# A fixed order of instructions for the attention stage of a hybrid encoder layer

## The chip, the cores and the metric

One NeuronCore of a Trainium2 chip. The metric is the device time of one execution in microseconds (us), the median of several executions. The engines are TensorE (PE in the profile; PEld is its weight load), VectorE (DVE), ScalarE (ACT), GpSimd (POOL), and SyncE (SP), which issues most of the transfers. Each has an instruction queue of its own, and they wait for each other through semaphores.

## What is computed

One layer of an encoder over 256 frames of 2048 features, all in float32. The reference, cut to what matters here:

```python
proj = x @ w_in                       # q | k | v | u, 1024 columns each
attn = chunk_band_attention(q, k, v, rel_bias)   # 16 heads of 64
ssm  = s5_mixer(u, ...)               # 64 groups, a 64-dim complex diagonal state each
ssm  = gelu(ssm)
ssm  = ssm * sigmoid(ssm @ w_glu + b_glu)
mixed = concat([rms_norm(attn, g_attn), rms_norm(ssm, g_ssm)]) @ w_out
x = layer_norm(alpha * x + mixed)
gate = causal_depthwise_conv(x @ w_gate)
x = layer_norm(alpha * x + (gelu(gate) * (x @ w_val)) @ w_ffn_out)

# in chunk_band_attention, per head:
scores = q @ k.T * 64 ** -0.5 + bias  # banded by chunks of 64 frames
out    = softmax(scores) @ v
# in s5_mixer, per group: s[t] = a * s[t-1] + B u[t] (complex, a scan); y = Re(C s) + D u
```

## The kernel before

All products run on TensorE as float32 matmuls of a rounded high part and a low rest. The weights come in chunks of 128 x 1024 elements (512 KB). The loop in `run` takes one chunk per step, and such a step is called a block below. For block j it first splits the weights of block j + 3 (`split_chunk`, lines 163 and 164: a cast on ScalarE gives hi, a subtraction on VectorE gives lo), then issues the transfer of block j + 7 on SP (`dma_chunk`), then the matmuls of block j, then what takes the result out of PSUM (`post`), and last one step of every side generator that has started, in the order in which they were registered. There are four buffers each for raw, hi and lo.

The blocks of the first phase: 0 to 7 half of V (`mm_b`, twelve matmuls of 512 columns a block, lines 245, 247, 249), 8 to 23 U (`mm_a`, eight pairs of one matmul of 512 and one of 256 columns, lines 206 to 211), 24 to 31 the other half of V, 32 to 63 K and Q (four blocks for each pair of heads: two of K, two of Q), 64 to 79 the attention half of the output projection (oa), 80 to 87 GLU, 88 to 103 the other half of it (os). Then comes the feed-forward part, which is most of the time and isn't touched.

The side generators that matter:

- `s5_loc` (from block 16) puts state products (ll, line 778) and transposes (lt, line 762) into a queue, each with a cost. `fill`, called after most matmuls, adds 1 to a credit (at most 2) and takes from the queue while the credit is at least 1. A state product costs 0.25, so a few of them go between two matmuls.
- `s5_kstack` (from 24) puts 64 products for the kernel matrix (ks, line 873) there, at 0.5 each, into PSUM bank 2, which half of V also uses.
- `s5_cm` (from 22) builds the matrices CM on VectorE (lines 943 to 948), two steps for each of four.
- `s5_scan` (from 35) runs the scan on VectorE: 21 complex multiply-adds of four operations each (lines 844 to 847), 14 of them long (128 x 512) and 7 short (128 x 64). `paced` emits one and yields when the costs reach a budget of 1.6 per block. Then `s5_y` (lines 952 to 983) makes y on TensorE (line 973), four times two halves of one PSUM bank, each copied out by VectorE (line 974), then the GELU and the operand of GLU.
- `attention(j)` (from block 36 + 4j, j from 0 to 7): the loads of the two bands of bias, the scores of two heads (S, lines 1048 and 1049), `soft` for each head (sum and maximum on VectorE, line 1061; their negative, line 1062; exponentials on ScalarE, line 1065), `trans` (three transposes and a copy to the one pT buffer on ScalarE, lines 1071 to 1075), `pv` (products with V, lines 1084 to 1086), `norm` (lines 1090 to 1099: reciprocal and product at on VectorE, then two squares on ScalarE), and `evac` (transposes back, line 1104; scaling and attnhl on ScalarE, lines 1108 and 1109; the low part on VectorE, line 1110).

`evac_k` (line 501, kz) and `evac_q` (line 506, qt) take K and Q out of PSUM, with a copy on ScalarE first (lines 467 and 469).

What is written isn't yet the order on an engine. The framework collects the instructions, and its scheduler lets each engine take, in a time that it assumes, the earliest-written instruction that is ready. So an engine's queue may differ from the written order. On the chip, each queue then runs in the order that was set.

Of the kernel before, what the change touches and what calls it, by code (L numbers as in the profile page):

```python
# [12 lines left out]
F32 = mybir.dt.float32  # L13
# [3 lines left out]
ALU = mybir.AluOpType  # L17
# [3 lines left out]
P = 128  # L21
# [97 lines left out]
class Builder:  # L119
    def __init__(self, nc, tc, ctx, I, out):  # L120
        self.nc, self.tc, self.ctx, self.I, self.out = nc, tc, ctx, I, out
        self.chunks = []
        self.sides = []
        self.queue = deque()
        self.credit = 0.0


# [39 lines left out]
    def run(self, first=None):  # L167
        self.raw, self.hl = {}, {}
        if first is not None:
            first()  # L170
        else:
            for j in range(4):
                self.dma_chunk(j)
            for j in range(3):
                self.split_chunk(j)
                self.dma_chunk(j + 4)
        self.start()
        j = 0
        while j < len(self.chunks) or self.sides:
            self.split_chunk(j + 3)  # L180
            self.dma_chunk(j + 7)
            if j < len(self.chunks):
                hi, lo = self.hl.pop(j)
                self.chunks[j][1](hi, lo)
                if self.chunks[j][2] is not None:
                    self.chunks[j][2]()
            keep = []
            for s in self.sides:
                if s[0] <= j:
                    try:  # L190
                        with self.tc.high_priority(s[2]) if s[2] else nullcontext():
                            next(s[1])
                    except StopIteration:
                        continue
                keep.append(s)
            self.sides = keep
            j += 1


    def mm_a(self, ps, hi, lo, xs, k0, first, last, nk=8):  # L200
# [49 lines left out]
                self.fill()  # L250

    def t1(self, shape, name):
        return self.ap_.tile(shape, F32, tag="t1", bufs=6, name=name)

    def bank(self, i, name):
        return self.pp.tile([P, 512], F32, tag=f"b{i}", name=name)
# [35 lines left out]
    def plan_phase1(self):  # L292
# [163 lines left out]
        self.side(24, self.s5_kstack(), 200)  # L456
        self.side(22, self.s5_cm())
        self.side(35, self.s5_scan())
        for j in range(8):
            self.side(36 + 4 * j, self.attention(j))  # L460
        self.side(78, self.load_x())
# [290 lines left out]
    def s5_loc(self):  # L752
        nc, bp = self.nc, self.bp
        loc, put = self.loc, self.put
        st = {}

        def lt(pg, ri):
            def mm(i):
                if i == 0:
                    st[0] = self.bank((6, 7)[ri], f"lt{pg}{ri}")  # L760
                c = pg * 8 + 2 * i
                nc.tensor.transpose(st[0][:, P * i:P * i + P],
                                    self.MB[:, ri, c:c + 2].rearrange("p c e q -> p (c e q)"), self.ident)

            def evac():
                for g2 in range(2):
                    r = slice(64 * g2, 64 * g2 + 64)
                    nc.scalar.copy(loc[r, pg % 2, ri, :, r], st[0][r].rearrange("p (i n) -> p i n", n=64))
            for i in range(4):
                put(lambda i=i: mm(i))  # L770
            put(evac, 0)

        def ll(q, ri):
            def mm(i, g2):
                if i == 0 and g2 == 0:
                    st[1] = self.bank((3, 4)[ri], f"ll{q}{ri}")
                r = slice(64 * g2, 64 * g2 + 64)
                nc.tensor.matmul(st[1][r, 64 * i:64 * i + 64], lhsT=loc[:, q % 2, ri, i, r], rhs=self.up[:, q * 8 + i],
                                 start=True, stop=True, tile_position=(0, 64 * g2))

            def evac():
                v = st[1].rearrange("p (i c) -> p i c", c=64)
                nc.scalar.copy(self.X[:, ri, q * 8:q * 8 + 8, 8:64], v[:, :, 0:56])
                nc.scalar.copy(self.L8[:, ri, q * 8:q * 8 + 8], v[:, :, 56:64])
            for i in range(8):
                for g2 in range(2):
                    put(lambda i=i, g2=g2: mm(i, g2), 0.25)
            put(evac, 0)

        def both(f, pg):  # L790
            for ri in range(2):
                f(pg, ri)

        def drained():
            while self.queue:
                yield
            yield
        for pg in range(2):
            while self.mb_ready <= pg:
                yield  # L800
            yield
            both(lt, pg)
            yield
        while self.mb_ready < 4 or self.up_ready < 1:
            yield
        self.X = bp.tile([P, 2, NP_, 64], F32, tag="d2", name="X")
        nc.gpsimd.memset(self.X[:, :, :, 0], 0.0)
        yield from drained()
        yield
        both(ll, 0)  # L810
        both(lt, 2)
        yield from drained()
        both(ll, 1)
        both(lt, 3)
        yield from drained()
        self.lt_done = True
        while self.up_ready < 2:
            yield
        yield
        both(ll, 2)  # L820
        both(ll, 3)
        yield from drained()
        self.loc_done = True
        yield

    def s5_scan(self):
# [8 lines left out]
        def madd(cost, o, s, ar, ai, shape, add=None):  # L835

            n = math.prod(shape[1:])
            add = o if add is None else add

            def f():  # L840
                u, w = (self.kcm[:, c:c + n].rearrange("p (r x) -> p r x", r=2) for c in (1024, 1536))
                if len(shape) == 4:
                    u, w = (t.rearrange("p r (c b) -> p r c b", b=shape[3]) for t in (u, w))
                V.tensor_tensor(u, s[:, ::-1], ai, op=ALU.mult)
                V.tensor_tensor(w, s, ar, op=ALU.mult)
                V.tensor_tensor(u, u, add, op=ALU.add)
                V.tensor_tensor(o, w, u, op=ALU.add)
            ops.append((cost, f))
        sh = [P, 2, NP_, 8]
        one = lambda q, k: q[:, :, :, k]  # L850
        bc = lambda q, k: one(q, k).unsqueeze(3).broadcast_to(sh)
        row = lambda k: L8 if k == 8 else X[:, :, :, k]
        for k in range(2, 9):
            madd(2.7, row(k), row(k - 1), bc(QR, 0), bc(QI, 0), sh)
        for b in range(7):
            madd(1.1, X[:, :, :, 0, b + 1], X[:, :, :, 0, b], one(QR, 7), one(QI, 7), [P, 2, NP_], L8[:, :, :, b])
        for k in range(1, 8):
            madd(2.7, row(k), row(0), bc(QR, k - 1), bc(QI, k - 1), sh)
        yield from self.paced(ops, 1.6)
        yield from self.s5_y()  # L860

    def s5_kstack(self):
# [5 lines left out]

        def mm(i, ri, h):
            if not st:  # L870
                st[0] = self.bank(2, "ks")
            pr = 16 * h + i
            nc.tensor.matmul(st[0][64 * h:64 * h + 64, 32 * i:32 * i + 32],
                             lhsT=self.MB[:, ri, pr].rearrange("p e q -> p (e q)"),
# [2 lines left out]
        for i in range(16):  # L877
            for ri in range(2):
                for h in range(2):
                    self.put(lambda i=i, ri=ri, h=h: mm(i, ri, h), 0.5)  # L880
        while self.queue:
            yield
        ps = st[0]
# [152 lines left out]
    def attention(self, j):  # L1036
# [2 lines left out]
        v = self.res1  # L1039
        st = {}  # L1040

        def load(h):
            b = st["b", h] = ap.tile([P, 256], F32, tag="band", bufs=2, name=f"bd{j}{h}")
            nc.sync.dma_start(b, I["band"][2 * j + h])

        def scores(h):
            ps = st["S", h] = self.bank(5 + h, f"S{j}{h}")
            nc.tensor.matmul(ps[:, 0:256], lhsT=qt[:, P:2 * P], rhs=kz[h], start=True, stop=True)
# [1 line left out]

        def soft(h):

            ps, b = st["S", h], st["b", h]
            s = ap.tile([P, 384], F32, tag="sT", bufs=2, name=f"sT{j}{h}")
            if h == 0:
                st["m"] = ap.tile([P, 12], F32, tag="mx", bufs=2, name=f"mx{j}")
# [10 lines left out]

        def trans(h):
            s = st["s", h]
            ps = self.bank(7, f"T{j}{h}")  # L1070
            nc.tensor.transpose(ps[:, 0:128], s[:, 256:384], self.ident)
            nc.tensor.transpose(ps[:, 128:256], s[:, 0:128], self.ident)
            nc.tensor.transpose(ps[:, 256:384], s[:, 128:256], self.ident)
            pt = st["pt", h] = ap.tile([P, 384], F32, tag="pT", name=f"pT{j}{h}")
            nc.scalar.copy(pt, ps[:, 0:384])

        def pv(h):
# [10 lines left out]
        def norm():  # L1088
            m = st["m"]
            nc.vector.reciprocal(m[:, 0:4], m[:, 8:12])  # L1090
            if j == 0:
# [1 line left out]
            a = st["a"] = self.t1([P, SEQ], f"at{j}")  # L1093
            nc.vector.tensor_tensor(a.rearrange("p (g c) -> p g c", c=64), st["o"][:, 0:256].rearrange("p (g c) -> p g c", c=64),
                                    m[:, 0:4].unsqueeze(2).broadcast_to([P, 4, 64]), op=ALU.mult)
            q = self.t1([P, SEQ], f"aq{j}")
            for t in range(2):
                r = slice(P * t, P * t + P)
                nc.scalar.activation(q[:, r], a[:, r], AF.Square, accum_out=self.ssq[:, t, j:j + 1])
# [1 line left out]
        def evac():  # L1101
# [5 lines left out]
            a = self.t1([P, SEQ], f"ag{j}")  # L1107
            nc.scalar.mul(a, ps, self.pv["g_attn"][:, j:j + 1])
            nc.scalar.copy(self.attnhl[:, j, 0:SEQ], a)
            nc.vector.tensor_tensor(self.attnhl[:, j, SEQ:], a, self.attnhl[:, j, 0:SEQ].bitcast(F32), op=ALU.subtract)  # L1110

        load(0)
        load(1)
        scores(0)
        scores(1)
        yield
        soft(0)
        yield
        soft(1)
        yield  # L1120
        if j < 7:
            yield
        trans(0)
        yield
        pv(0)
        trans(1)
        if j < 7:
            yield
        pv(1)
        norm()  # L1130
        yield
        while self.cm_ready < 4:
            yield
        evac()
        yield


# [251 lines left out]
```

## Time and profile before

| | |
|---|---|
| median of 3 runs | 1140.65 us (1139.38 to 1142.46) |
| profiled execution, its own time | 1141.15 us |
| its span, first to last instruction | 1139.3 us |
| TensorE busy | 1110.3 us (97%) |
| VectorE busy | 774.4 us (68%) |
| ScalarE busy | 566.6 us (50%) |
| GpSimd busy | 75.5 us (7%) |
| mean granted TensorE clock | 0.991 |

The busy time of an engine is a share of the whole span, over stages with different limits. The granted clock is the share of the full TensorE clock that the chip allowed. The times of matmuls overlap, so what one takes is read from start to start.

### The profile page before, as it was taken

The numbers are of one execution on the slowest core, as the hardware profiler recorded it, in microseconds if no ns is written. First come the engines' busy times: TensorE is split into PE (matmuls) and PEld (weight loads), VectorE is DVE, ScalarE is ACT, GpSimd is POOL, SyncE is SP. The second block draws the span as 40 slices with busy tenths as digits, with TensorE's granted clock in tenths as the row PEclk, the third lists the DMA queues.
The fourth block names the chain that finished last, engine by engine and source line by source line (L and its number), as shares of the span: only waits on it lengthen the run. The fifth ranks groups of instructions, "written<-read, shape, count | busy, mean of one in ns | idle before, by whom it ended". The sixth has DMA issues, their size and how long they took to land.

```text
span 1139.3 us, 17905 instructions
## 1 busy us (share of the span) xinstructions
PE 1110.3 (97%) x6980; PEld 948.8 (83%) x6980; DVE 774.4 (68%) x1230; ACT 566.6 (50%) x882; POOL 75.5 (7%) x75
## 2 busy tenths in 40 slices
PE   8999979999999999999999999999999999999996
PEld 6887768888887888888888888888888888888885
DVE  7996889946588776666666666666666575454555
ACT  5455325537575565555555555555555443433350
POOL 2021300000011000000000000000000550000002
PEclk9999979999999999999999999999999999999998
DMA  8886334534766366666666666666666876666661
GB/s 303 279 226 164 118 122 139 162 96 138 244 188 201 108 204 186 185 188 185 188 188 188 186 187 186 186 185 185 189 186 187 307 223 197 190 198 190 192 195 74
DMA packets 61572, 212.03 MB, mean 186 GB/s; under 512 B 7344, under 2 KB 10800, under 8 KB 60592
## 3 DMA queue, kind: packets, MB, share of 16 engines
q1 hardware_dynamic: 59728, 204.18, 58.9%
q0 software_dynamic: 1472, 6.29, 1.8%
q8 instruction: 54, 0.88, 0.3%
q10 hardware_dynamic: 288, 0.43, 0.1%
q14 instruction: 30, 0.25, 0.1%
HBM read 207.46 MB, written 3.41 MB: 185 GB/s over the span
## 4 chain that ended last, share of the span: by engine, by line
PE 93%; DVE 4%; ACT 1%; issue 1%; DMA 1%; SPq 0%; POOL 0%; ACTq 0%; POOLq 0%
PE f L231 29%; PE f L224 15%; PE d L245 7%; PE d L249 7%; PE d L247 7%; PE kq L209 5%; PE u L209 2%; PE kq L211 2%; PE oa L249 1%; PE oa L245 1%; PE oa L247 1%; PE u L211 1%; PE glu L209 1%; DVE lo L164 1%; PE os L249 1%; PE os L245 1%
## 5 line engine op out<-in xcount | busy, mean ns | idle before, releaser
L164 DVE TENSOR_TENSOR lo<-raw,hi 128x1024 fp32r<-128x1024 f32 (+1 forms) x358 | 446.3, 1249 | 210.6 <-ACT hi L163 207.0
L163 ACT CAST hi<-raw 128x1024 fp32r<-128x1024 f32 (+1 forms) x358 | 374.3, 1047 | 300.0 <-PE d L249 116.9
L231 PE MATMUL f<-x1s,hi 128*128 128x512 f32 (+1 forms) x1408 | 487.2, 396 | 1.5 <-DVE x1s L1211 1.5
L224 PE MATMUL f<-x1s,lo 128*128 128x256 f32 x1408 | 380.0, 281 | 0.0
L231 PEld LDWEIGHTS f<-x1s,hi 128*128 128x128 f32 x1408 | 258.8, 188 | 57.6 <-DVE x1s L1211 1.8
L224 PEld LDWEIGHTS f<-x1s,lo 128*128 128x128 f32 x1408 | 265.8, 189 | 8.6
L247 PE MATMUL d<-lo,hid 128*128 128x512 f32 (+1 forms) x360 | 133.4, 371 | 0.0
L245 PE MATMUL d<-hi,hid 128*128 128x512 f32 (+1 forms) x360 | 133.4, 370 | 0.0
L249 PE MATMUL d<-hi,hid 128*128 128x512 f32 (+1 forms) x360 | 133.3, 370 | 0.0
L209 PE MATMUL kq<-xs,hi 128*128 128x512 f32 x240 | 92.8, 422 | 5.1 <-DVE qt L506 2.6
L247 PEld LDWEIGHTS d<-lo,hid 128*128 128x128 f32 x360 | 67.9, 188 | 11.7
L249 PEld LDWEIGHTS d<-hi,hid 128*128 128x128 f32 x360 | 67.8, 188 | 11.7
L245 PEld LDWEIGHTS d<-hi,hid 128*128 128x128 f32 x360 | 67.9, 188 | 11.5
L211 PE MATMUL kq<-xs,lo 128*128 128x256 f32 x240 | 69.8, 291 | 0.0
L209 PEld LDWEIGHTS kq<-xs,hi 128*128 128x128 f32 x240 | 47.0, 196 | 15.8 <-DVE qt L506 2.7
L1319 ACT COPY ga<-f 128x256 f32<-128x256 f32 x44 | 16.4, 372 | 83.3 <-PE f L231 83.3
L1326 DVE TENSOR_TENSOR gp<-f,ga 128x256 f32<-128x256 f32 x44 | 18.8, 426 | 45.6 <-ACT ga L1319 45.6
L1319 ACT COPY va<-f 128x256 f32<-128x256 f32 x44 | 16.4, 372 | 66.1 <-PE f L231 66.1
L1338 DVE TENSOR_TENSOR va<-f,va 128x256 f32<-128x256 f32 x44 | 18.7, 425 | 43.0 <-ACT va L1319 43.0
L211 PEld LDWEIGHTS kq<-xs,lo 128*128 128x128 f32 x240 | 47.2, 197 | 0.8
L209 PE MATMUL u<-xs,hi 128*128 128x512 f32 x120 | 43.5, 401 | 0.0
L1305 POOL DMA_DIRECT2D gb<-rows x4 | 2.2, 554 | 531.6 <-PE f L231 531.6
(228 smaller groups left out, 1366.9 us busy)
## 6 DMA issues: line engine op xcount, KB each, us to landing
raw<-wf SPq DMA_DIRECT2D x176, 512.0 KB, 3.7
raw<-wd SPq DMA_DIRECT2D x88, 512.0 KB, 4.1
raw<-wkq SPq DMA_DIRECT2D x32, 512.0 KB, 3.7
raw<-wo SPq DMA_DIRECT2D x32, 512.0 KB, 4.0
raw<-wu SPq DMA_DIRECT2D x16, 512.0 KB, 4.7
raw<-wv SPq DMA_DIRECT2D x15, 512.0 KB, 6.2
raw<-wg SPq DMA_DIRECT2D x8, 512.0 KB, 3.7
gb<-rows POOLq DMA_DIRECT2D x4, 1024.0 KB, 13.1
```

Of the source, the lines that this page charges most:

```text
L163: self.nc.scalar.copy(hi[:, c], raw[:, c])
L164: self.nc.vector.tensor_tensor(lo[:, c], raw[:, c], hi[:, c].bitcast(F32), op=ALU.subtract)
L209: nc.tensor.matmul(ps, start=first and kk == 0, stop=False, **h)
L211: nc.tensor.matmul(ps[:, 0:SEQ], start=False, stop=False, **l)
L224: nc.tensor.matmul(th(ps), lhsT=lo[:, w], rhs=th(x), start=False, stop=False)
L231: nc.tensor.matmul(ps[:, c], lhsT=hi[:, w], rhs=x[:, c], start=start and part is None, stop=stop)
L245: nc.tensor.matmul(ps, lhsT=ah, rhs=wh, start=first and kk == 0, stop=False)
L247: nc.tensor.matmul(ps, lhsT=ah, rhs=wl, start=False, stop=False)
L249: nc.tensor.matmul(ps, lhsT=al, rhs=wh, start=False, stop=last and kk == 1)
L1319: self.nc.scalar.copy(tv, v[:, :, 1])
L1326: nc.vector.tensor_tensor(g[:, 2:].rearrange("p (t c) -> p t c", t=2), p0, t, op=ALU.add)
L1338: nc.vector.tensor_tensor(tv, p0, tv, op=ALU.add)
```

## The change

- `keep_order` is called after each block of the first phase. It gives every instruction of TensorE that was written in blocks 26 to 73, and every one of VectorE and ScalarE written in blocks 33 to 73, an edge to the one written before it on the same engine, with no semaphore. Within these blocks the engines keep the written order.
- State products and the products of the kernel matrix cost 0 in the queue, so each lot runs at once; the third and the fourth lot of state products are drained one by one. The kernel matrix goes to bank 0.
- The scan is emitted operation by operation (0.68 for a long one, 0.28 for a short one), with 1.5 of credit per block.
- Attention: scores and both heads' `soft` in the first step, both `trans` two blocks later (into banks 7 and 6, or 4 for the last), with two pT buffers, `pv` and `norm` a block behind that, `evac` two blocks later, and its subtraction another block later (for the last j both without the extra block). The bands of the next j are loaded after `soft`; the first ones by a side generator from block 30.
- The squares write into the buffer of the first head's probabilities; the shared buffers t1 are five instead of six.

```diff
@@ run
         while j < len(self.chunks) or self.sides:
+            self.j = j
...
             self.sides = keep
+            if first is not None:
+                self.keep_order(26 <= j < 74, 33 <= j < 74)
             j += 1
+
+    def keep_order(self, pe, others):
+
+        new, mark = [], self.mark
+        for i in reversed(self.nc.cur_bb.bb.instructions):
+            if i is mark:
+                break
+            new.append(i)
+        if new:
+            self.mark = new[0]
+        E = mybir.EngineType
+        for i in reversed(new):
+            if pe and i.engine == E.PE or others and i.engine in (E.DVE, E.Activation):
+                prev = self.last.get(i.engine)
+                if prev is not None:
+                    self.tc.add_manual_dep(i, prev, mybir.DependencyInfo(
+                        mybir.DependencyClass.NoSync, mybir.DependencyReason.DATA), reason="order")
+                self.last[i.engine] = i.name
@@ t1
-        return self.ap_.tile(shape, F32, tag="t1", bufs=6, name=name)
+        return self.ap_.tile(shape, F32, tag="t1", bufs=5, name=name)
@@ plan_phase1
+        self.side(30, self.first_band())
@@ s5_loc
-                    put(lambda i=i, g2=g2: mm(i, g2), 0.25)
+                    put(lambda i=i, g2=g2: mm(i, g2), 0)
...
         both(ll, 2)
+        yield from drained()
         both(ll, 3)
@@ s5_scan, madd
-                V.tensor_tensor(u, s[:, ::-1], ai, op=ALU.mult)
-                V.tensor_tensor(w, s, ar, op=ALU.mult)
-                V.tensor_tensor(u, u, add, op=ALU.add)
-                V.tensor_tensor(o, w, u, op=ALU.add)
-            ops.append((cost, f))
+                return ((u, s[:, ::-1], ai, ALU.mult), (w, s, ar, ALU.mult), (u, u, add, ALU.add), (o, w, u, ALU.add))
+            for i in range(4):
+                def g(i=i):
+                    d, a, b, op = f()[i]
+                    V.tensor_tensor(d, a, b, op=op)
+                ops.append((cost, g))
...
-        yield from self.paced(ops, 1.6)
+        have = 0.0
+        for cost, f in ops:
+            while have < cost:
+                yield
+                have += 1.5
+            f()
+            have -= cost
+        yield
@@ s5_kstack
-                st[0] = self.bank(2, "ks")
+                st[0] = self.bank(0, "ks")
...
-                    self.put(lambda i=i, ri=ri, h=h: mm(i, ri, h), 0.5)
+                    self.put(lambda i=i, ri=ri, h=h: mm(i, ri, h), 0)
@@ attention
-            ps = self.bank(7, f"T{j}{h}")
+            ps = self.bank((7, 6 if j < 7 else 4)[h], f"T{j}{h}")
...
-            pt = st["pt", h] = ap.tile([P, 384], F32, tag="pT", name=f"pT{j}{h}")
+            pt = st["pt", h] = ap.tile([P, 384], F32, tag="pT", bufs=2, name=f"pT{j}{h}")
...
-            q = self.t1([P, SEQ], f"aq{j}")
+            q = st["s", 0]
...
             nc.scalar.copy(self.attnhl[:, j, 0:SEQ], a)
+            if j < 7:
+                yield
             nc.vector.tensor_tensor(self.attnhl[:, j, SEQ:], a, self.attnhl[:, j, 0:SEQ].bitcast(F32), op=ALU.subtract)
 
-        load(0)
-        load(1)
         scores(0)
         scores(1)
-        yield
         soft(0)
-        yield
         soft(1)
-        yield
+        if j < 7:
+            self.load_band(j + 1)
+        yield
+        yield
+        trans(0)
+        trans(1)
+        yield
+        pv(0)
+        pv(1)
+        norm()
+        yield
+        assert self.cm_ready == 4
         if j < 7:
             yield
-        trans(0)
-        yield
-        pv(0)
-        trans(1)
-        if j < 7:
-            yield
-        pv(1)
-        norm()
-        yield
-        while self.cm_ready < 4:
-            yield
-        evac()
+        yield from evac()
```

## Rows read from the trace of the kernel before

**Rows 1.** Timeline of PE, first K and first GLU matmuls: start, duration, line.
```profile
108.41 0.39 PE L209 MATMUL kq<-xs,hi 128*128 128x512 f32 x1
...
314.64 0.39 PE L209 MATMUL glu<-ssmhl,hi 128*128 128x512 f32 x1
...
315.33 0.40 PE L209 MATMUL glu<-ssmhl,hi 128*128 128x512 f32 x1
```
**Rows 2.** Busy time by stretch: length, engines' busy us, PEclk, DMA share, GB/s.
```profile
108.00:315.00 207.00, 196.93 (x1958) 166.80 (x1957) 152.97 (x309) 103.09 (x222) 9.23 (x7) 0.97 0.47 146
140.00:180.00 40.00, 31.61 (x171) 26.30 (x170) 35.44 (x85) 15.29 (x37) 0.00 (x0) 0.83 0.43 127
180.00:222.50 42.50, 42.50 (x267) 37.93 (x267) 41.89 (x96) 24.93 (x65) 0.00 (x0) 1.00 0.52 161
```
**Rows 3.** Waits from 140 to 180 us: total us, times, longest.
```profile
PE kq L209 <- DVE qt L506: 2.6, 1, 2.6
PE kq L209 <- DVE kz L501: 2.5, 2, 2.1
PE T L1071 <- ACT sT L1065: 2.4, 2, 2.0
```
**Rows 4.** Busy time by stretch, behind one of the waits.
```profile
165.70:170.50 4.80, 4.80 (x15) 4.12 (x16) 3.87 (x8) 0.00 (x0) 0.00 (x0) 0.50 0.09 33
```
**Rows 5.** Timeline of PE, the first scores of two successive attention steps.
```profile
193.80 0.60 PE L1048 MATMUL S<-kz,qt 128*128 128x256 f32 x2
...
208.48 0.60 PE L1048 MATMUL S<-kz,qt 128*128 128x256 f32 x2
```
**Rows 6.** Timeline of PE, state products in a run, and alternating (first, and what follows).
```profile
84.88 2.08 PE L778 MATMUL ll<-up,loc 128*64 128x64 f32 x64
...
118.91 0.56 PE L778 MATMUL ll<-up,loc 128*64 128x64 f32 x10
...
130.63 0.50 PE L209 MATMUL kq<-xs,hi 128*128 128x512 f32 x1
```
**Rows 7.** Timeline of PE, the kernel matrix, with the idle time before it.
```profile
109.29 3.93 PE L873 MATMUL ks<-scb,MB 128*64 128x32 f32 x128 [0.49 <-ACT vtok L362]
```
**Rows 8.** Timeline of DVE, the last step of two successive attentions.
```profile
193.08 0.42 DVE L1110 TENSOR_TENSOR attnhl<-ag,attnhl 128x256 fp32r<-128x256 f32 x1
...
207.43 0.42 DVE L1110 TENSOR_TENSOR attnhl<-ag,attnhl 128x256 fp32r<-128x256 f32 x1
```
**Rows 9.** Groups of DVE between these: busy, mean ns, idle before and releaser.
```profile
L844 DVE TENSOR_TENSOR kcm<-X,QI 128x512 f32<-128x512 f32 x3 | 2.1, 690 | 0.0
...
L506 DVE SCALAR_TENSOR_TENSOR qt<-kq,qb 128x256 f32<-128x256 f32 x1 | 0.4, 425 | 0.2 <-ACT qb L469 0.2
```
**Rows 10.** Timeline of ACT, first and last of the squares of one attention.
```profile
189.21 0.31 ACT L1099 ACTIVATE aq<-at 128x128 f32<-128x128 f32 x1 [1.10 <-DVE at L1094]
...
189.72 0.19 ACT L1099 ACTIVATION_READ_ACCUMULATOR aq<-at 128x1 f32 x1
```
**Rows 11.** Costliest groups of the page, the hi cast.
```profile
L163 ACT CAST hi<-raw 128x1024 fp32r<-128x1024 f32 (+1 forms) x358 | 374.3, 1047 | 300.0 <-PE d L249 116.9
```
**Rows 12.** Timeline of ACT, first and last of one head's exponentials.
```profile
226.01 0.51 ACT L1065 ACTIVATE sT<-sT,mx 128x256 f32<-128x256 f32 x1 [1.67 <-DVE mx L1062]
...
226.81 0.19 ACT L1065 ACTIVATION_READ_ACCUMULATOR sT<-sT,mx 128x1 f32 x1
```
**Rows 13.** Timeline, a copy of y, the other half's first matmuls, what follows it.
```profile
237.01 0.60 DVE L974 COPY ysh<-y 128x256 f32<-128x256 f32 x1
...
237.66 0.37 PE L973 MATMUL y<-up,Kt 128*32 128x64 f32 x8 [0.18 <-DVE ysh L974]
...
239.24 0.50 PE L209 MATMUL kq<-xs,hi 128*128 128x512 f32 x1
```
**Rows 14.** Timeline of PE, the wait at the start of the feed-forward stage.
```profile
393.05 0.39 PE L231 MATMUL f<-x1s,hi 128*128 128x256 f32 x1 [1.53 <-DVE x1s L1211]
```
**Rows 15.** Busy time by stretch, around that wait.
```profile
392.00:396.00 4.00, 2.95 (x24) 2.96 (x25) 3.20 (x6) 4.00 (x13) 0.00 (x0) 1.00 0.00 0
```

More of the change, by code (lines that the diff above doesn't have):

```diff
@@ L124, in __init__ @@
         self.queue = deque()
+        self.mark, self.last = None, {}
         self.credit = 0.0
@@ L853, in s5_scan @@
         for k in range(2, 9):
-            madd(2.7, row(k), row(k - 1), bc(QR, 0), bc(QI, 0), sh)
+            madd(0.68, row(k), row(k - 1), bc(QR, 0), bc(QI, 0), sh)
         for b in range(7):
-            madd(1.1, X[:, :, :, 0, b + 1], X[:, :, :, 0, b], one(QR, 7), one(QI, 7), [P, 2, NP_], L8[:, :, :, b])
+            madd(0.28, X[:, :, :, 0, b + 1], X[:, :, :, 0, b], one(QR, 7), one(QI, 7), [P, 2, NP_], L8[:, :, :, b])
         for k in range(1, 8):
-            madd(2.7, row(k), row(0), bc(QR, k - 1), bc(QI, k - 1), sh)
-        yield from self.paced(ops, 1.6)
+            madd(0.68, row(k), row(0), bc(QR, k - 1), bc(QI, k - 1), sh)
+        have = 0.0
[6 more added lines that the diff above has]
+        yield
         yield from self.s5_y()
@@ L1040, in attention @@
         st = {}
-        def load(h):
-            b = st["b", h] = ap.tile([P, 256], F32, tag="band", bufs=2, name=f"bd{j}{h}")
-            nc.sync.dma_start(b, I["band"][2 * j + h])
         def scores(h):
@@ L1051, in soft @@
         def soft(h):
-            ps, b = st["S", h], st["b", h]
+            ps, b = st["S", h], self.band[j, h]
             s = ap.tile([P, 384], F32, tag="sT", bufs=2, name=f"sT{j}{h}")
@@ L1109, in evac @@
             nc.scalar.copy(self.attnhl[:, j, 0:SEQ], a)
+            if j < 7:
+                yield
             nc.vector.tensor_tensor(self.attnhl[:, j, SEQ:], a, self.attnhl[:, j, 0:SEQ].bitcast(F32), op=ALU.subtract)
-        load(0)
-        load(1)
         scores(0)
         scores(1)
+        soft(0)
+        soft(1)
+        if j < 7:
+            self.load_band(j + 1)
         yield
-        soft(0)
         yield
-        soft(1)
-        yield
-        if j < 7:
-            yield
         trans(0)
+        trans(1)
         yield
         pv(0)
-        trans(1)
-        if j < 7:
-            yield
         pv(1)
@@ L1131, in attention, with load_band, first_band @@
         yield
-        while self.cm_ready < 4:
+        assert self.cm_ready == 4
+        if j < 7:
             yield
-        evac()
+        yield from evac()
+    def load_band(self, j):
+        for h in range(2):
+            b = self.band[j, h] = self.ap_.tile([P, 256], F32, tag="band", bufs=2, name=f"bd{j}{h}")
+            self.nc.sync.dma_start(b, self.I["band"][2 * j + h])
+    def first_band(self):
+        self.band = {}
+        self.load_band(0)
         yield
```

## The prediction

> **What bounds the kernel now.** I read the busy times by stretch first. The change acts between the first K projection matmul at 108.41 us and the first GLU matmul at 314.64 [rows 1], so the stretch that counts is 206.2 us long, and TensorE is busy in 196.9 of 207 us there [rows 2]. The losses are in one place: from 140 to 180 us TensorE is busy in 31.6 of 40 us at a mean granted clock of 0.83, while VectorE is busy in 35.4. From 180 to 222.5 TensorE has no idle time, and VectorE is busy in 41.9 of 42.5 us [rows 2]. The waits of TensorE in the bad stretch come second: for qt, for kz and for the exponentials sT, 7.5 us together [rows 3]. All are late VectorE and ScalarE work of the attention: scan and CM work stand on VectorE ahead of them. Third the clock: after these waits TensorE works at 0.50 of its full clock, the 1.2 GHz level, for 4.8 us in one such stretch [rows 4]; there are two, and each loses half of what it lasts, 2.4 us. So the disorder costs some 8.4 + 4.8 = 13 us. It isn't a lack of capacity, since the regular stretch behind it runs without a gap.
>
> I count in blocks (one 512 KB weight chunk each), and a round is four blocks, K and Q of two heads with one attention step. From scores to scores a round takes 208.48 - 193.80 = 14.68 us [rows 5], and it is TensorE's own work. Two pairs of projection matmuls take 315.33 - 314.64 = 0.69 us [rows 1], one 0.345, so a block is 8 x 0.345 = 2.8 us, four are 11.2, and attention is the other 3.4.
>
> **State products in runs.** 64 of their instructions take 2.08 us in a run; the 128 that alternate with projection matmuls take 130.63 - 118.91 = 11.72 us [rows 6], of which 15 projection matmuls are about 2.6, so 9.1 against 4.2. That gives 4.9, and half as much, 2.5, for the 64 spread over the value stage in the same pattern: 7.4 us. A gain below zero is excluded, since the run is measured in this kernel; if the next operation absorbs part, it is less, down to nothing. The kernel matrix (ks) costs 3.9 us at either place; its wait of 0.5 for vtok goes with the bank [rows 7]. It and 64 more state products come before the K stage now, so this begins at 108.4 - 2.5 + 3.9 + 2.1 = 111.9 us.
>
> **Stated order.** From block 26 on TensorE, and from 33 on VectorE and ScalarE, each engine runs strictly as emitted, up to block 73. TensorE then loses what it waits for, and no later work fills in. First it runs ahead: three rounds (the first without attention, with 2.1 of state products) are 11.2 + 2.1 + 2 x 14.7 = 42.7, with 1.3 of first waits 44.0, up to 155.9 us.
>
> Then VectorE decides. Between two attnhl subtractions, 207.43 - 193.08 = 14.35 us, it stood still for 0.2 only, with ten scan operations [rows 8, 9]. The new pace, 1.5 of credit per block at 0.68 an operation, is 8.8 per round. At some 0.62 us from start to start (the row's 0.69 overlaps the next by 0.08), this saves 0.75: 14.35 - 0.2 - 0.75 = 13.4. But the stated order adds two waits on VectorE per round, both for ScalarE. After the normalisation (at) ScalarE has two squares, 0.7 us [rows 10], ahead of the next hi cast, 1.05 us [rows 11], and VectorE's next instruction is the lo subtraction of that cast: 1.8 us. After the second head's maxima ScalarE has that head's exponentials, 1.0 us [rows 12], the end of the first head's and again a cast, and VectorE again stands at a lo: 2.2 us. What is queued behind: the scan, kz and qt, and TensorE waits for qt with the scores. A round becomes 13.4 + 4.0, about 17.5 with a late -max, 2.8 over TensorE's 14.7. The bounds of the waits are 0 (the row of before, where other work fills) and 4.0; I take 4.0, since both engines are now in order and the chain is from rows. Five rounds (blocks 44 to 63): 87.5, up to 243.4 us.
>
> The tail, blocks 64 to 79: sixteen blocks of 12 x 0.23 = 2.75, 44.0; the eighth attention, 3.4; eight halves of y at 239.24 - 237.66 = 1.6 [rows 13], 12.6. The waits: 2.0 of the last scores for qt, 1.4 of its transposes and products, 2.9 of the first y for the last scan operation (block 66, which VectorE reaches late: soft, at, both waits, four lo and nine scan operations are 15.3 us since qt, TensorE's work is 12.4), and four y halves that wait for the copy of the other half in their bank. That copy was bridged before by projection matmuls, 0.2 us of wait beside a copy of 0.6 [rows 13]; now nothing may go between, 0.2 to 0.9 each, and I take 0.8: 3.2. One lo behind the GELU, 1.0. Sum 70.5, up to 313.9 us against 314.6 before: **0.7 us gained**.
>
> So the change takes back 13 us of disorder and 7.4 of alternation, and pays five times 2.8 and 10.5 in the tail, less the 5 or so of waits and switching that y had before.
>
> **At nothing.** The band loads move behind soft on SP: a raw load behind them has three blocks, some 8 us, of cover; without it one landing would show. Transposes a block later and two pT buffers: the products waited 0.6 once; covered now by a block, 2.8 us. Five t1 buffers instead of six in GLU: the nearest row is the wait of 1.53 at a later stage's start [rows 14], so 0 to 1.5; I take 0, as a block sets its buffers free again. The scan emitted operation by operation costs no more instructions. Squares written into sT delay only the next round's soft, which is later anyway.
>
> **Sum.** The profiled execution took 1141.15 us, of which 1139.3 are span; it stands 0.5 over the median of 1140.65. 1141.15 - 0.7 = 1140.4, against the median 1140.0: **no change that can be told**, 0.3% being 3.4 us, about what a measurement of this kernel can tell from no change.
>
> **Rivals.**
> A, the two waits don't bind: casts run earlier, or VectorE keeps its lead, and rounds stay at 14.7. For it: 13.4 is below 14.7, and rounds without a gap exist [rows 2, 5]. Against it: a strict queue has nothing to put into 4.0 us. It saves 5 x 2.8 and the first y's 2.9: 1140.0 - 17 = 1123 us.
> B, the order isn't what is emitted, and operations still move where it matters: then only the runs pay, 7.4 us: 1133 us. Against it: each instruction gets an edge to the one before on its engine.
> C, slower: the clock falls in the tail. There TensorE's own work is the bound, and waits of 2.0 and 2.9 us stand near each other, at blocks 64 and 67, about as long as the waits of 2.6 and 2.1 before the two half-clock stretches of before [rows 3, 4]. Each fall costs 2.4 us, two 4.8, and as much again if y's four waits prolong it: 1145 to 1150, say 1146. In the rounds before, a fall is paid out of the 2.8 us in which TensorE waits anyway, so it decides only from the second in one round, or in the tail. Against it: a wait of 1.53 us left the clock at 1.00 [rows 14, 15]. The Trainium skill (TensorE: Matmul & The Clock Gate, "Part 1: The HAM clock gate") says that "the default state is throttled, and activity releases the throttle". By that rule any long enough wait puts the half rate back, and the sum would be C's; the rows show both outcomes, so I leave it a rival.
>
> **How the numbers follow.** My forecast 0.48, A 0.17, B 0.10, C 0.25. The forecast's own range is 1135 to 1146 (the waits 0.5 either way per round, the y halves, alternation): 0.30 within 0.3%, 0.09 on each side. A and most of B are faster, C mostly slower. Faster 0.34, same 0.36, slower 0.30. The range reaches half way into A and to C's end: 1128 to 1150.
>
> **What would show it.** Right: state products in runs of 64 instructions; lo subtractions that wait for hi twice per round, about 1.8 and 2.2 us; scores that wait for qt by 1 to 2 us from the third attention on; rounds of 17 to 18 us between scores; y halves that wait 0.8 for ysh; no projection matmul between them. Wrong: rounds of 14.7 us (A), scan operations that are bunched (B), a granted clock under 1 after 240 us (C), or a new wait outside of blocks 26 to 79, which I have at nothing.

## The result, and the profile after

The changed kernel takes **1148.18 us** (median of 5) against 1140.85: ratio 1.006, interval 1.0042 to 1.0078. A repetition on another occasion gave 1147.69, ratio 1.0064 (1.0051 to 1.0077). It is slower by 0.6%, about 7 us. The time lies inside the range, but the forecast was no change, and slower had 0.30. Two of the five executions, one of them the profiled one, ran at a mean granted clock of 0.557 and 0.848 (1818.48 and 1219.77 us) and are left out of the ratio, so the lines below are from the repetition: own time 1145.70 us, span 1143.9, the lowest of its runs (1145.70 to 1149.19).

The place is the one that the prediction named, and it can be dated. Timeline of PE, the first scores of attentions 0 to 7 (start, duration, line, and in brackets the idle time before and its releaser):

```profile
129.47 0.67 PE L1076 MATMUL S<-kz,qt 128*128 128x256 f32 x2 [1.32 <-DVE qt L529]
...
145.46 0.70 PE L1076 MATMUL S<-kz,qt 128*128 128x256 f32 x2 [0.85 <-DVE qt L529]
...
163.59 0.70 PE L1076 MATMUL S<-kz,qt 128*128 128x256 f32 x2 [0.92 <-DVE qt L529]
...
181.72 0.70 PE L1076 MATMUL S<-kz,qt 128*128 128x256 f32 x2 [1.64 <-DVE qt L529]
...
199.64 0.70 PE L1076 MATMUL S<-kz,qt 128*128 128x256 f32 x2 [1.04 <-DVE qt L529]
...
216.90 0.70 PE L1076 MATMUL S<-kz,qt 128*128 128x256 f32 x2 [0.76 <-DVE qt L529]
...
234.89 0.70 PE L1076 MATMUL S<-kz,qt 128*128 128x256 f32 x2 [1.57 <-DVE qt L529]
...
253.03 0.80 PE L267 MATMUL oa<-hi,attnhl 128*128 128x512 f32 x1 [3.77 <-DVE qt L529]
...
257.04 0.91 PE L1076 MATMUL S<-kz,qt 128*128 128x256 f32 x2
```

Read the distances: 16.0, 18.1, 18.1, 17.9, 17.3, 18.0 and 22.1 us, where a round of before took 14.68 [rows 5]. In front of all but the last TensorE waits for qt. In the last distance the wait is at block 64, 3.77 us: this block (oa) takes banks 0 and 1, and bank 1 still holds the last Q until qt is taken out of it. There is a second wait in each round, in front of the transposes T, for the exponentials sT; waits of PE from 100 to 345 us (total, times, longest):

```profile
PE S L1076 <- DVE qt L529: 8.1, 7, 1.6
PE T L1099 <- ACT sT L1093: 5.8, 12, 1.2
```

What holds VectorE up stands in one round. Timeline, the ScalarE and VectorE lines put in order of time:

```profile
146.92 0.42 DVE L1122 TENSOR_TENSOR at<-O,mx 128x256 f32<-128x256 f32 x1
147.44 0.31 ACT L1127 ACTIVATE sT<-at 128x128 f32<-128x128 f32 x1 [6.25 <-DVE at L1122]
...
148.04 1.04 ACT L164 CAST hi<-raw 128x1024 fp32r<-128x1024 f32 x1
149.11 1.23 DVE L165 TENSOR_TENSOR lo<-raw,hi 128x1024 fp32r<-128x1024 f32 x1 [1.77 <-ACT hi L164]
...
153.52 0.17 DVE L1090 TENSOR_SCALAR mx<-mx 128x2 f32<-128x2 f32 x1
...
154.76 1.03 ACT L164 CAST hi<-raw 128x1024 fp32r<-128x1024 f32 x1
155.82 1.23 DVE L165 TENSOR_TENSOR lo<-raw,hi 128x1024 fp32r<-128x1024 f32 x1 [2.12 <-ACT hi L164]
```

ScalarE is idle 6.25 us in front of the squares: they wait for at, and the cast that VectorE wants next stands behind them. At the second lo, the cast stands behind the exponentials. 1.77 and 2.12 us, against 1.8 and 2.2 worked out from rows 10 to 12. The waits of VectorE from 145.4 to 253 us show that nothing else stops it there, two waits in each of six rounds:

```profile
DVE lo L165 <- ACT hi L164: 22.7, 12, 2.1
```

The answers to rows 2 and 4, busy time by stretch, and to rows 6 and 13, timeline:

```profile
140.00:180.00 40.00, 35.98 (x216) 30.14 (x214) 31.61 (x65) 18.01 (x46) 0.00 (x0) 1.00 0.45 135
180.00:222.00 42.00, 36.55 (x215) 30.71 (x215) 31.59 (x83) 18.45 (x49) 0.00 (x0) 1.00 0.42 135
...
253.00:257.00 4.00, 3.97 (x9) 3.14 (x10) 2.20 (x5) 1.63 (x5) 0.00 (x0) 0.50 0.37 131
```
```profile
111.65 0.39 PE L231 MATMUL kq<-xs,hi 128*128 128x512 f32 x1
111.97 2.08 PE L801 MATMUL ll<-up,loc 128*64 128x64 f32 x64
...
270.23 0.37 PE L1005 MATMUL y<-up,Kt 128*32 128x64 f32 x8 [0.71 <-DVE ysh L1006]
...
320.38 0.39 PE L231 MATMUL glu<-ssmhl,hi 128*128 128x512 f32 x1
```

From 140 to 180 us the change is a gain: 36.0 us busy at a granted clock of 1.00, against 31.6 at 0.83 [rows 2]. From 180 on it gives that back: 36.55 of 42 us busy, where before had no gap at all, and VectorE is busy in 31.6 of 42 instead of 41.9 of 42.5. Both engines are idle, which says that the order and not the load is at fault. State products run 64 at a time, the K stage begins at 111.65, and the first GLU matmul starts at 320.38, 5.7 us later than before [rows 1]. Over the whole execution the two profiles lie 4.6 us apart (1145.70 and 1141.15). The medians lie about 7 apart; where the rest is lost, no profile shows.

### The profile page after: what moved, and what is told of

It reads as the page before. It is cut to its first block, busy times and chain, and to the rows that moved or that the text cites. A ratio compares the mean times of both kernels' runs of the same rounds, so it can differ in the third digit from the quotient of the medians.

```text
span 1816.7 us, 17906 instructions
## 1 busy us (share of the span) xinstructions
PE 1797.9 (99%) x6980; PEld 1241.3 (68%) x6980; DVE 775.0 (43%) x1230; ACT 566.4 (31%) x880; POOL 71.1 (4%) x75
## 4 chain that ended last, share of the span: by engine, by line
PE 99%; DVE 1%; DMA 0%; ACT 0%; issue 0%; SPq 0%; ACTq 0%
PE f L253 29%; PE f L246 15%; PE d L269 7%; PE d L267 7%; PE d L271 7%; PE kq L231 5%; PE kq L233 3%; PE u L231 3%; PE v L269 1%; PE v L271 1%; PE v L267 1%; PE os L269 1%; PE os L267 1%; PE oa L269 1%; PE oa L267 1%; PE oa L271 1%
## 5 line engine op out<-in xcount | busy, mean ns | idle before, releaser
L253 PE MATMUL f<-x1s,hi 128*128 128x512 f32 (+1 forms) x1408 | 761.7, 569 | 0.5 <-DVE x1s L1246 0.5
L246 PE MATMUL f<-x1s,lo 128*128 128x256 f32 x1408 | 524.4, 385 | 0.0
L253 PEld LDWEIGHTS f<-x1s,hi 128*128 128x128 f32 x1408 | 308.7, 222 | 192.5 <-issue 93.5
L246 PEld LDWEIGHTS f<-x1s,lo 128*128 128x128 f32 x1408 | 316.5, 225 | 34.5 <-issue 11.6
L269 PE MATMUL d<-lo,hid 128*128 128x512 f32 (+1 forms) x360 | 195.3, 542 | 0.0
L271 PE MATMUL d<-hi,hid 128*128 128x512 f32 (+1 forms) x360 | 195.2, 542 | 0.0
L267 PE MATMUL d<-hi,hid 128*128 128x512 f32 (+1 forms) x360 | 194.7, 541 | 0.0
L231 PE MATMUL kq<-xs,hi 128*128 128x512 f32 x240 | 137.2, 589 | 0.0
L267 PEld LDWEIGHTS d<-hi,hid 128*128 128x128 f32 x360 | 81.7, 227 | 48.9 <-issue 28.1
L271 PEld LDWEIGHTS d<-hi,hid 128*128 128x128 f32 x360 | 81.3, 226 | 48.6 <-issue 28.1
L231 PE MATMUL u<-xs,hi 128*128 128x512 f32 x120 | 67.8, 582 | 0.0
L233 PE MATMUL u<-xs,lo 128*128 128x256 f32 x120 | 47.3, 394 | 0.0
```

The source lines that it names most:

```text
L231: nc.tensor.matmul(ps, start=first and kk == 0, stop=False, **h)
L233: nc.tensor.matmul(ps[:, 0:SEQ], start=False, stop=False, **l)
L246: nc.tensor.matmul(th(ps), lhsT=lo[:, w], rhs=th(x), start=False, stop=False)
L253: nc.tensor.matmul(ps[:, c], lhsT=hi[:, w], rhs=x[:, c], start=start and part is None, stop=stop)
L267: nc.tensor.matmul(ps, lhsT=ah, rhs=wh, start=first and kk == 0, stop=False)
L269: nc.tensor.matmul(ps, lhsT=ah, rhs=wl, start=False, stop=False)
```

## The experiments

| kernel | us | ratio to before, interval |
|---|---|---|
| changed, repeated | 1147.69 | 1.0064 (1.0051 to 1.0077) |
| order on TensorE alone | 1129.83 | 0.9908 (0.9894 to 0.9922) |
| no order | 1129.06 | 0.9900 (0.9885 to 0.9915) |
| before, with the runs only | 1129.68 | 0.9908 (0.9894 to 0.9921) |
| ScalarE free | 1121.62 | 0.9839 (0.9823 to 0.9856) |
| VectorE free | 1125.63 | 0.9870 (0.9856 to 0.9885) |
| lo a block later | 1132.48 | 0.9929 (0.9913 to 0.9945) |
| last Q in another bank | 1148.39 | 1.0075 (1.0060 to 1.0090) |
| squares a block later | 1135.47 | 0.9965 (0.9950 to 0.9979) |
| exponentials a block later | 1132.11 | 0.9929 (0.9914 to 0.9944) |
| both a block later | 1123.01 | 0.9855 (0.9841 to 0.9870) |
| ScalarE free, y in two banks | 1120.59 | 0.9832 (0.9818 to 0.9847) |

All compute the whole layer.

**The changed kernel, repeated.**

> The changed kernel as it is, for a profile at the full TensorE clock. Measured so far: 1148.2 us against 1140.9. Theory V (VectorE's two waits for ScalarE per round of four blocks, put there by the fixed order): rounds between scores of 17.5 us or more from the third attention on, over 18 if V also has to explain the 8 us by which the forecast fell short; scores wait for qt. Theory C (the clock falls behind waits): rounds near 17.5, and granted clock clearly below 1 in stretches between 240 and 300 us. Theory T (TensorE's own order costs it: y halves, transposes and products of which each now waits in line): rounds of 15 to 16 us, and waits of 10 us and more in the tail.

Rounds of 17.9 on average from the second scores to the seventh, (234.89 - 145.46) / 5, with VectorE's two waits: V, though not the over 18 by which V was to explain the whole loss from the rounds. The rest stands in the first rounds and at block 64. For C there is one stretch at 0.50, behind the wait of 3.77 us. T's waits are small: the halves of y wait 2.8 us together.

**Which engine's order costs.** Two edits of one line:

```diff
-                self.keep_order(26 <= j < 74, 33 <= j < 74)
+                self.keep_order(26 <= j < 74, False)      # order on TensorE alone
+                pass                                       # no order
```

> The changed kernel, with the written order kept on TensorE alone; VectorE and ScalarE are ordered by the scheduler as before. Theory V: the two waits per round go, 1125 to 1135 us. Theory T: stays at 1145 or more. Theory C: follows whatever the waits of TensorE become, and would show in the granted clock.

> The changed kernel without any edge of order; the moved steps, the buffers and the runs stay. If the order is the whole cost, the runs pay: 1130 to 1136 us. If the moved steps, five t1 buffers or the pacing cost something by themselves: 1141 or more.

1129.8 and 1129.1 us, the second 1 us under its range. The order on VectorE and ScalarE costs 18 us, the one on TensorE nothing that shows. The moved steps, the buffers and the pacing together don't cost either: without any order the kernel is 11 us faster than before, as is the kernel before with the runs alone, below. T falls.

**The runs alone.**

```diff
-                    put(lambda i=i, g2=g2: mm(i, g2), 0.25)
+                    put(lambda i=i, g2=g2: mm(i, g2), 0)
...
-                st[0] = self.bank(2, "ks")
+                st[0] = self.bank(0, "ks")
...
-                    self.put(lambda i=i, ri=ri, h=h: mm(i, ri, h), 0.5)
+                    self.put(lambda i=i, ri=ri, h=h: mm(i, ri, h), 0)
```

> The kernel before, with only the state products and the kernel matrix in runs (costs of 0, the third and fourth lot drained one by one, the kernel matrix in bank 0). By the sum of the prediction 7.4 us less plus 0.5 for the wait for vtok: 1133 us. If the time of alternation is absorbed by the disorder behind it: 1139 to 1141.

1129.7: 10.9 us gained, more than the 7.9 expected. Most of it isn't gained where the alternation was: the first scores come only 1.1 us earlier than before (140.93 against 142.03), the first GLU matmul 11.9 us earlier (302.77 against 314.64). The bad stretch of before is nearly gone by itself, busy time by stretch in this kernel:

```profile
140.00:180.00 40.00, 39.07 (x231) 34.65 (x232) 39.14 (x106) 20.63 (x54) 0.00 (x0) 0.96 0.48 151
```

39.07 of 40 us against 31.61 [rows 2]; in exchange some 5.5 us of waits come up from 110 to 145 us, where before had none. So a good part of the disorder went with this edit, which the prediction had priced as separate. How the two are linked wasn't tried.

**ScalarE or VectorE.**

```diff
-            if pe and i.engine == E.PE or others and i.engine in (E.DVE, E.Activation):
+            if pe and i.engine == E.PE or others and i.engine == E.DVE:           # ScalarE free
+            if pe and i.engine == E.PE or others and i.engine == E.Activation:    # VectorE free
```

> The changed kernel with the order kept on TensorE and VectorE, ScalarE left to the scheduler. Theory V (VectorE stands at a lo subtraction while ScalarE has squares or exponentials ahead of the cast): the cast can go ahead of them, so most of the 18 us that the order on both engines costs come back: 1128 to 1135. Rival W (it is VectorE's own written order that costs, scan operations ahead of qt and kz): 1143 or more.

> The changed kernel with the order kept on TensorE and ScalarE, VectorE left to the scheduler. Theory V: VectorE fills its two waits with scan operations, 1128 to 1135. Theory W: the same, since its order is gone. If it stays at 1143 or more, the order on ScalarE is the cost by itself. Together with the run that frees ScalarE alone it tells V from W.

1121.6 and 1125.6 us, both better than V had it. With VectorE still in its written order the kernel is 26 us faster than the changed one, so W falls: it is not where the scan stands ahead of qt. With ScalarE still in order and VectorE free it is 22 us faster, so the order on ScalarE alone isn't the cost either: it takes both. The trace of the run with ScalarE free shows what moved, in the timeline of both engines:

```profile
185.54 1.04 ACT L164 CAST hi<-raw 128x1024 fp32r<-128x1024 f32 x1
188.34 0.42 DVE L1122 TENSOR_TENSOR at<-O,mx 128x256 f32<-128x256 f32 x1
188.69 1.22 DVE L165 TENSOR_TENSOR lo<-raw,hi 128x1024 fp32r<-128x1024 f32 x1
188.80 0.31 ACT L1127 ACTIVATE sT<-at 128x128 f32<-128x128 f32 x1 [2.22 <-DVE at L1122]
```

The cast is done ahead of the squares, and lo starts directly behind at. From 145.4 to 234 us VectorE waits for a cast once, 0.5 us, where the changed kernel waits ten times. A round is 14.78 us, (218.46 - 144.58) / 5, timeline of PE:

```profile
144.58 0.59 PE L1076 MATMUL S<-kz,qt 128*128 128x256 f32 x2
...
218.46 0.59 PE L1076 MATMUL S<-kz,qt 128*128 128x256 f32 x2
```

It also beats the kernel without any order, with intervals that don't overlap: a written order on TensorE and VectorE is worth having.

**The lo subtraction a block later, in full order.** One cast is always done before VectorE comes to its lo:

```diff
-                self.nc.vector.tensor_tensor(lo[:, c], raw[:, c], hi[:, c].bitcast(F32), op=ALU.subtract)
+                f = lambda c=c: self.nc.vector.tensor_tensor(lo[:, c], raw[:, c], hi[:, c].bitcast(F32), op=ALU.subtract)
+                self.late.append(f)
+                if not self.lag:
+                    self.drain_late()
...
+            self.drain_late()
+            self.lag = first is not None and 33 <= j < 74
             self.split_chunk(j + 3)
-            self.dma_chunk(j + 7)
+            while sent <= j + 7 - self.lag:
+                self.dma_chunk(sent)
+                sent += 1
```

> The changed kernel with its order kept on all three engines; only the lo subtraction of a weight block is written one block later than its cast, in blocks 33 to 73 (the transfer behind it one block later as well). Nothing is left out. Theory V: the waits of 1.7 and 2.1 us on VectorE go, rounds between scores fall from 17.9 to 14.7 to 15.2, the wait for qt at block 64 shrinks: 1124 to 1131. Theory W, or a cost of any fixed order: 1140 or more.

1132.5: 15 us less than the changed kernel, but 1.5 over V's range. The rounds do what V says, 15.26 us, (220.84 - 144.56) / 5:

```profile
144.56 0.70 PE L1089 MATMUL S<-kz,qt 128*128 128x256 f32 x2
...
220.84 0.70 PE L1089 MATMUL S<-kz,qt 128*128 128x256 f32 x2 [0.24 <-DVE qt L542]
```

What is missing stands behind the rounds, waits of PE from 100 to 345 us:

```profile
PE oa L280 <- DVE qt L542: 2.5, 1, 2.5
PE oa L280 <- ACT hi L164: 2.3, 1, 2.3
```

The first is at block 64 (236.32 us); the second, at 290.15 us, is a new wait for a cast, near the end of the ordered blocks; the transfers were a block later here too. Its cause wasn't tried. Behind both the granted clock was at 0.50, from 236 to 241 and from 290 to 293 us.

**The last Q in another bank.**

```diff
-                        cur["ps"] = self.bank(c // 2, f"kq{j}{c}")
+                        cur["ps"] = self.bank(3 if (j, c) == (7, 2) else c // 2, f"kq{j}{c}")
```

> The changed kernel with the last Q projection (blocks 62 and 63) in bank 3 instead of bank 1, so that block 64, which takes banks 0 and 1, needn't wait for qt. If the wait of 3.8 us there and the half-clock stretch behind it (4 us at 0.50) are an own cost: 4 to 5 us less, 1143 to 1144, and no granted clock under 1 between 240 and 300 us. If the wait only moves to the scores behind block 64, nothing: 1147.

1148.4: nothing gained; the intervals of this and the changed kernel overlap. The wait at block 64 is gone and the clock stays at 1.00 there, but TensorE now waits behind it, timeline of PE, and then busy time by stretch:

```profile
253.09 0.70 PE L1076 MATMUL S<-kz,qt 128*128 128x256 f32 x2 [1.71 <-DVE qt L529]
...
267.67 0.43 PE L1005 MATMUL y<-X,vtok 128*32 128x64 f32 x16 [2.28 <-DVE X L872]
...
280.47 0.45 PE L1005 MATMUL y<-up,Kt 128*32 128x64 f32 x8 [1.43 <-issue]
```
```profile
280.50:283.50 3.00, 3.00 (x53) 2.63 (x53) 0.61 (x1) 0.82 (x3) 0.00 (x0) 0.50 0.17 67
```

The second is the wait of the first y for the last scan operation. VectorE's lag is the cost, and a freed bank only moves the place where it is paid: the wait at block 64 isn't an own cost. For the half clock the run decides nothing. It was to be free of clocks under 1 from 240 to 300 us, and wasn't: one half-clock stretch went, and another came, behind an idle time without a releaser that the profile shows. What the one in the changed kernel costs can be read from its lines: nine products of block 64 take 257.04 - 253.03 = 4.0 us, where at the prediction's 0.23 each they take 2.1. So C is in the loss with some 2 us, an estimate, but behind a wait that VectorE's lag made; the two kernels in which this lag is gone, ScalarE free and both moves below, have a granted clock of 1.00 from 140 to 330 us.

**One wait at a time, in full order.** The squares, and the exponentials, each written behind the next cast:

```diff
         norm()
         yield
+        squares()      # squares a block later; norm keeps reciprocal and product
...
             self.load_band(j + 1)
         yield
+        exps(0)        # exponentials a block later; soft keeps sum, maximum, negative
+        exps(1)
         yield
         trans(0)
```

> The changed kernel with its order kept on all three engines; the two squares of an attention step on ScalarE are written one block later, behind the next hi cast. Theory V: the wait of 1.7 us per round on VectorE goes and that of 2.1 stays; rounds fall from 17.9 to about 16.2, six of them give 10 us: 1136 to 1140. If the two waits aren't separate costs (the other takes over what the one gives back): 1145 or more.

> The changed kernel with its order kept on all three engines; the exponentials of both heads are written one block later, behind the next hi cast and a block ahead of their transposes. Theory V: the wait of 2.1 us per round goes and that of 1.7 stays; rounds of about 15.8, 12 us less: 1133 to 1138. If the transposes then wait for the exponentials instead: 1143 or more, with T waiting for sT by 2 us a round.

> Both moves, the order kept on all three engines. Theory V: VectorE has no wait of a round left, rounds are TensorE's 14.7, the scores' wait for qt and that of block 64 go: 1121 to 1127. If a fixed order costs by itself: above 1130.

1135.5, 1132.1 and 1123.0 us: 12, 16 and 25 less than the changed kernel, the first two just below V's ranges and the third inside. First and last scores of five rounds, timelines of the three kernels: (226.94 - 146.38) / 5 = 16.11, (222.35 - 144.44) / 5 = 15.58 and (218.22 - 144.84) / 5 = 14.68.

```profile
146.38 0.70 PE L1076 MATMUL S<-kz,qt 128*128 128x256 f32 x2 [0.86 <-DVE qt L529]
...
226.94 0.70 PE L1076 MATMUL S<-kz,qt 128*128 128x256 f32 x2 [1.23 <-DVE qt L529]
```
```profile
144.44 0.59 PE L1076 MATMUL S<-kz,qt 128*128 128x256 f32 x2
...
222.35 0.59 PE L1076 MATMUL S<-kz,qt 128*128 128x256 f32 x2
```
```profile
144.84 0.59 PE L1076 MATMUL S<-kz,qt 128*128 128x256 f32 x2
...
218.22 0.59 PE L1076 MATMUL S<-kz,qt 128*128 128x256 f32 x2
```

17.89 less 1.78 and less 2.31: each move takes its own wait out of the round, and VectorE's waits for hi show the other still there, from 145.4 to 234 us, and below them the waits of PE for these two inputs, from 100 to 345 us (total, times, longest). First the kernel with the squares moved, then that with the exponentials moved:

```profile
DVE lo L165 <- ACT hi L164: 10.3, 5, 2.1
PE S L1076 <- DVE qt L529: 7.3, 7, 1.4
```
```profile
DVE lo L165 <- ACT hi L164: 10.6, 6, 1.8
PE T L1102 <- ACT sT L1097: 3.3, 9, 0.9
PE S L1076 <- DVE qt L529: 1.3, 1, 1.3
```

So the two waits of VectorE reach TensorE at different places. With the squares moved the transposes no longer wait for sT and the scores still wait for qt; with the exponentials moved the scores wait only once, before the first attention, and the transposes still wait. With both moved only that first 1.3 is left of the two, and a round is exactly the 14.68 of before's good stretch. A fixed order on three engines isn't slow; this one had two groups of instructions in front of a cast that was needed sooner.

**y in two banks**, on top of ScalarE free:

```diff
-            ps = self.bank((3, 4)[pg % 2], f"y{pg}")
             for f in range(2):
+                ps = self.bank(3 + f, f"y{pg}{f}")
```

> The best so far (order on TensorE and VectorE, ScalarE left to the scheduler, 1121.6), with the two halves of each y product in different PSUM banks. The four waits of 0.7 us of the second half for the copy of the first go: 2 to 3 us less, 1118.5 to 1119.5. If the next block's products take the wait over (their bank is read a block before): 1121 to 1122.

1120.6, between the two expectations; the ratios 0.9832 and 0.9839 can't be told apart. The wait for the copy is gone from TensorE's list, but other idle time stands beside y in its place, waits of PE from 100 to 345 us, without a releaser that the profile shows:

```profile
PE y L1005 <- issue: 2.3, 1, 2.3
PE oa L271 <- issue: 1.7, 1, 1.7
```

This and the kernel with ScalarE free are the fastest of the study, 1.6 to 1.7% under before; the interval of the fully ordered kernel with both moves, 1.4% under, overlaps with that of ScalarE free.

## Why the prediction was wrong

The **mechanism** was right, and the sum had it too small. The forecast put the first GLU matmul at 313.9 us; it came at 320.38, so a gain of 0.7 became a loss of 5.7 there. Step by step:

- **State products in runs**: right. The K stage began at 111.65 us, forecast 111.9. As a part alone, with the kernel matrix, they are worth 10.9 us rather than 7.9, as most of the disorder behind them goes too.
- **"First it runs ahead: three rounds"**: this step failed first. VectorE had no lead to use up: its first wait for a cast behind the exponentials, 2.12 us, comes already in the first attention (lo at 138.03 us), not after three rounds. Block 44 was to begin at 155.9 and began at 159.60, 3.7 us late; with both groups moved the scores behind it come at 159.61 instead of 163.59. The three blocks by which the weights run ahead don't help, because what is late is qt and sT.
- **"Then VectorE decides"**: right. The two waits were 1.77 and 2.12 where 1.8 and 2.2 stood. The five rounds up to block 64 took 248.32 - 159.60 = 88.7 us where 87.5 was forecast: a mis-sizing of 1.2. Taking 4.0 of the bounds 0 to 4.0 was right for this order, and the runs that move the squares, the exponentials or both show each part of it.
- **"The tail"**: the step left out that block 64 takes the bank of the last Q. It took 320.38 - 248.32 = 72.1 us where 70.5 was forecast, 1.6 too long. At block 64 stood a wait of 3.77 and some 2 us of half clock, where the last scores were to wait 2.0. Against that, the 2.9 of the first y for the scan didn't come, because the wait had been paid already; with the bank freed, 2.28 of it came. Nor did the 1.4 for the last transposes and products. The halves of y waited 0.71 where 0.8 was taken.
- **"How the numbers follow"**: 3.7, 1.2 and 1.6 make the 6.5 us by which the GLU was late, all on one side. The chance for slower was hung on C, and the mechanism of the forecast itself, a few us larger, made most of the miss. That the time still lies in the range is owed to C's end of it: the forecast's own range ended at 1146.

The block starts, timeline of PE:

```profile
159.60 0.48 PE L231 MATMUL kq<-xs,hi 128*128 128x512 f32 x1
...
248.32 0.47 PE L267 MATMUL oa<-hi,attnhl 128*128 128x512 f32 x1
```

Rival A, rounds of 14.7, is what the order would have given with the cast in front, 1123 by its working and 1123.0 measured with both moved; the place agrees too, the first GLU matmul at 297.32 us where A's 16.9 less make 297.0. B, an order that doesn't hold, is refuted: VectorE's two waits stand in each of the six rounds. Of C one fall is there, by the prediction's own sign, a granted clock under 1 after 240 us: behind the wait of 3.77 us the clock was at 0.50, the 1.2 GHz level, for the 4 us looked at. It is worth some 2 us and not C's two falls. The waits of 0.76 to 1.64 us ahead of the scores left it at 1.00. By the rule of the Trainium skill (TensorE: Matmul & The Clock Gate, "Part 1: The HAM clock gate") idleness brings the half rate back; the trace agrees for the long wait and shows none for the short ones. The kernel with that bank freed has its fall elsewhere, and the same time, so what C costs by itself stays an estimate.

## What to carry to other kernels

Before instructions are fixed in a written order, go through each in-order queue and ask of every instruction that waits for another engine what stands behind it and who needs that first: here 0.6 us of squares held back a cast by the whole wait for their input. Put work that is ready, and that another engine will ask for, in front of work that waits for that engine. And when a stage turns from one engine's pace to another's, count every hand-over in the chain as busy time, and try a freed buffer only after the lag itself is gone.

## What had not been expected of the hardware

A wait of 3.77 us of TensorE was followed by a granted clock of 0.50 for at least 4 us, while waits of up to 1.64 us, one per 18 us, were not. The other runs show that the length of a wait alone doesn't sort the cases. Followed by 0.50 were 2.53 us (lo a block later), 1.84 (exponentials a block later), and 1.43 that came 0.9 us of products behind one of 0.74 (last Q in another bank); before, one of 2.6 us, and one of 2.1 right behind one of 2.0 [rows 3, 4]. Not followed by it were 2.28 (last Q in another bank) and 2.27 (y in two banks). What tells them apart wasn't tried.
